# Permuted tokens, densely written block transposes, and strip tiles moved into the closing sums' buffer, in a decoder layer on one Trainium2 core

## The chip, the cores and the metric

The kernel runs on one core of one Trainium2 chip. Its time is the device time of one launch in microseconds, and a kernel's time is the median of its runs. PE is the matmul engine, DVE and ACT the vector and the scalar engine, POOL the general engine, and SP here only issues DMAs. POOL and ACT issue DMAs too. Each engine works through its own queue of instructions in the order in which they were put there.

## The reference, cut to what matters

One layer of a decoder, 256 tokens of width 2048, all in float32:

```
h  = rmsnorm(x) ; p = h @ W_in                        # 2048 -> 3 x 1024 + 512 + 512 + 64
A  = 8 heads, causal dilated windows (128,1), (512,4), (2048,16), partial rotary, merged by softmax denominators
B  = 8 heads, latent attention with rotary part, causal
x  = x + rmsnorm(concat(A, B) @ W_out)
u  = square(relu(rmsnorm(x) @ W_up))                  # 2048 -> 8192
x  = x + rmsnorm(u @ W_down)                          # 8192 -> 2048
```

The gains of the norms are left out above. Positions enter through the rotary parts and the causal masks alone; everything else treats each token by itself.

## The kernel before, in words

**Matmuls.** The tokens form two blocks of 128 (`b` = 0, 1), one token per partition. Each float32 operand of a matmul is split into a high part (`hi`, an ACT copy that rounds, L310; for W_up with the gain, L314) and a low part (`lo`, the rest, on DVE, L311 and L315), and PE adds three products of 128x128 by 128x512 for each block of a product (L300). Weight tiles of 128x1024 arrive as `raw` by DMAs that SP issues (L194), and are split on ACT and DVE before PE uses them. Some pairs of row tiles go through a scheme of seven products instead of eight: POOL loads both tiles as one transfer of 1 MB (L378, into `ab`, `ab2`, later `ab_down`, `u` and `c`), DVE forms the sums of weights (L365 to L370, into `st_down`, `t`, `u`), and these too are split. The products go to banks `m` (up) or `md` (down).

**Up projection.** The outer loop has eight stages `j`; each makes 1024 columns of W_up's result for both blocks, that is, the strips 2j and 2j+1 of 512 columns. At a stage's end `close` (L1095 and L1098) turns the banks `m` into four tiles of 128x512 in the buffer `c` (the closing sums, 128x2048), which are then added to the four accumulators (L1160). In the next stage `up_evac` takes each accumulator: ACT applies relu and the square into a tile `r` (L941, L942; three buffers with the tag "r"), and a DMA on ACT's queue writes `r` to memory as `rkeep`, with its pieces permuted (L944). `turn_u` reads it back as `x` (L953, also in the "r" buffers), and DVE transposes it in blocks of 32x32 (STREAM_TRANSPOSE, L962) into `uT`, the transposed strip that the down projection uses on the stationary side. For strips 4 to 13, `lo_away` puts the low part of `uT` in memory ahead of time: ACT writes a negated rounded copy `neg` (L976, again in the "r" buffers), ACT's queue sends it to `ukeep` (L978), POOL later adds `uT` to it by an accumulating DMA (L988), and the down projection loads it as `ulo` (L1018).

**Down projection.** It starts at 707.7 us with strips that are ready, while the last strips are still being evacuated. For each strip, `uhi` and `ulo` are made by ACT and DVE (`split`, L310 and L311) or, for strips 4 to 13, by ACT (L1001) and the load. The seven-products steps load their weights into `ab_down`, `u` or `c`; `c`, the former closing buffer, is used by five of these loads, the first one soon after the start. Near the end `x_back` loads the residual x (`xkeep`) into the space of four old strips (L1212, four DMAs on SP) and scales it by `pwi` (L1217).

**The order.** A Python object (`Flow`) keeps a clock that advances with each matmul put into PE's queue. Work beside the matmuls is written as chains that give the number of units (us of that clock) until they go on; when the clock reaches a chain's due time, its next instructions are appended to their engines' queues. So delays in the code, such as `D_BACK`, `D_TURN` and `D_LO`, set places in the queues, not times on the chip. Weight tiles are appended so many tiles ahead of their use (`W_AHEAD` = 6).

```
nc.vector.transpose(uT[j][:, :, b * P:(b + 1) * P].rearrange("p k (t q) -> p k q t", q=4),
                    x.rearrange("p (q k c) -> p k q c", q=4, k=4))
if j in AWAY:
    flow.start(lo_away(j), 1.0)
```

Of the kernel before, what the change touches and what calls it, by code (L numbers as in the profile page):

```python
# [53 lines left out]

def shape_constants():

    fa = (THETA ** (-np.arange(0, RA, 2, dtype=np.float64) / RA)).astype(np.float32)
    fb = (THETA ** (-np.arange(0, RB, 2, dtype=np.float64) / RB)).astype(np.float32)
    freq = np.concatenate([-fa, fa, -fb, fb, fa, fa, fb, fb])
    i = np.arange(P)[:, None] + P  # L60
    j = np.arange(2 * P)[None, :]
    dist = i - j
    count = np.zeros((P, 2 * P))
    for window, dil in CONFIGS:
        count += (dist >= 0) & (dist <= window) & (dist % dil == 0)
    bias_a = np.where(count > 0, np.log(np.maximum(count, 1)) / SCALE_A, NEG)
    bias_b = np.where(dist >= 0, 0.0, NEG)
    out = np.concatenate([np.broadcast_to(freq, (P, 192)), bias_a, bias_b], axis=1)
    return np.ascontiguousarray(out.astype(np.float32))
# [24 lines left out]

D_BACK, D_LAST, D_TURN, D_LO, D_ADD = 12.0, 6.0, 9.0, 4.0, 23.0

# [171 lines left out]
def layer(nc, tc, io):  # L268
# [570 lines left out]
    pw, pwi = [con.tile([P, NB], F32, name=n) for n in ("pw", "pwi")]  # L839
    pws = con.tile([P, 4, NB], F32, name="pws")  # L840
    xkeep = [dram.tile([P, D], F32, name=f"xkeep{b}") for b in range(NB)]

    def powers():
# [11 lines left out]
        nc.vector.tensor_single_scalar(out=pwi.bitcast(I32), in_=pw.bitcast(I32), scalar=0x7F800000, op=OP.bitwise_xor)  # L855
        nc.vector.tensor_scalar_mul(pwi, pwi, 0.5)
        for i, (v, c) in enumerate(((pwi, 1.0 / D), (pwi, EPS), (pw, EPS))):
            nc.vector.scalar_tensor_tensor(out=pws[:, i, :], in0=v, scalar=c, in1=v, op0=OP.mult, op1=OP.mult)
# [78 lines left out]
    def up_evac(j, b, acc, order):  # L937
# [7 lines left out]
                            in_=r.rearrange("m (a c) -> m a c", a=4))  # L945
        flow.start(turn_u(j, b, keep), D_BACK + D_LAST * (b and j % 2))

    turned = set()

    def turn_u(j, b, keep):  # L950

        x = late["up"].tile([P, 512], F32, tag="r", bufs=3, name=f"x{j}_{b}")
        nc.scalar.dma_start(out=x, in_=keep)  # L953
        yield D_TURN
        if j not in uT:
            if j in (0, 1, 10, 11, 12, 13):
                t2 = late["u01" if j < 2 else "ab2" if j < 12 else "ab"][:, j % 2 * CW:(j % 2 + 1) * CW]
            else:
                tag = {"tag": "T", "bufs": 2} if j > 13 else {"tag": f"uT{j}", "bufs": 1}
                t2 = late["up"].tile([P, CW], F32, name=f"uT{j}", **tag)  # L960
            uT[j] = t2.rearrange("p (k s) -> p k s", k=4)
        nc.vector.transpose(uT[j][:, :, b * P:(b + 1) * P].rearrange("p k (t q) -> p k q t", q=4),  # L962
                            x.rearrange("p (q k c) -> p k q c", q=4, k=4))
        if b:
            turned.add(j)
            if j in AWAY:
                flow.start(lo_away(j), 1.0)

# [238 lines left out]
    def x_back():  # L1207

        for b in range(NB):
            for i in range(2):  # L1210
                x = uT[6 + 2 * b + i].rearrange("p k s -> p (k s)")
                nc.sync.dma_start(out=x, in_=xkeep[b][:, i * CW:(i + 1) * CW])  # L1212
        yield 20.0
        for b in range(NB):
            for i in range(2):
                x = uT[6 + 2 * b + i].rearrange("p k s -> p (k s)")
                nc.vector.tensor_scalar_mul(x, x, pwi[:, b:b + 1])  # L1217
                yield 1.5
# [117 lines left out]
def arrays_of(inputs):  # L1336

    a = {n: np.ascontiguousarray(inputs[n][0]) for n in ("x", "w_in", "w_uq", "w_ukv", "w_out", "w_up", "w_down")}
    a["xt"] = np.ascontiguousarray(np.concatenate([a["x"], inputs["norm_attn_pre"]]).T)
    a["pos"] = np.ascontiguousarray(inputs["positions"].reshape(NB, P).T)  # L1340
    a["gains"] = np.ascontiguousarray(np.concatenate(
# [3 lines left out]
    for n in ("norm_attn_post", "norm_mlp_post"):  # L1345
        a[n] = np.ascontiguousarray(inputs[n])
    a["consts"] = shape_constants()
    return a
# [20 lines left out]
```

## Time and profile before

| | us |
|---|---|
| runs | 1061.3, 1063.65, 1061.65 (median 1061.65) |
| profiled execution, its own time | 1060.02 |
| its span, first to last instruction | 1058.2 |
| busy: PE, DVE, ACT, POOL | 1030.5, 842.7, 638.7, 74.8 |
| mean granted clock of PE | 0.991 |

In rows of the profile, "out<-in" names what an instruction writes and reads, followed by its size; a bracket at a row's end gives the idle time of that engine just before it and what ended it. A row of a window's table gives the window, its length, and for PE, PEld (weight loads of PE), DVE, ACT and POOL the busy time with the count of instructions, then the granted clock, the share of busy DMA engines and GB/s. A row of waits gives engine and instruction, what it waited for, the total, how many times, and the longest. A row of a tile gives a form with its count, the least, median and largest duration in ns, and the first and last start. In a chain, start, length and what it was.

### The profile page before, as it was taken

What the parts mean: (1) busy time and instruction counts of PE and PEld (TensorE: products, weight loads), DVE (VectorE), ACT (ScalarE), POOL (GpSimd) and SP (SyncE); (2) the same over time, 40 slices, a digit from 0 to 9 for tenths busy, and PEclk for the clock granted to TensorE, in tenths of its full rate; (3) what the DMA queues carried; (4) which work ended last, traced back from release to release, by engine and by line L of the source; (5) the groups of instructions that cost most, each with busy time, mean ns of one, the idle gap of its engine ahead of it and who ended that gap; (6) DMA issues with size and microseconds to landing.
All of it is one profiled execution on the core that took longest, in us unless ns stands there. A gap on an engine that the chain in (4) does not pass through costs nothing.

```text
span 1058.2 us, 13302 instructions
## 1 busy us (share of the span) xinstructions
PE 1030.5 (97%) x4715; PEld 853.2 (81%) x4715; DVE 842.7 (80%) x1125; ACT 638.7 (60%) x862; POOL 74.8 (7%) x114
## 2 busy tenths in 40 slices
PE   9999999999999999999999999896999999999996
PEld 6888899888888788888887768685888888888885
DVE  6676546577556679999989889894999999989795
ACT  6675446565454567676575676665576665767561
POOL 0000000000000000000010100010210100121100
PEclk9999999999999999999999999998999999999998
DMA  8975547454356298777898988779979868889962
GB/s 303 363 232 151 147 122 229 149 170 156 123 197 221 92 366 264 233 258 231 271 275 270 307 236 270 208 266 328 310 268 379 299 216 302 284 312 328 365 235 80
DMA packets 108099, 259.74 MB, mean 245 GB/s; under 512 B 8704, under 2 KB 29696, under 8 KB 107648
## 3 DMA queue, kind: packets, MB, share of 16 engines
q1 hardware_dynamic: 64144, 169.90, 47.7%
q0 software_dynamic: 19072, 66.59, 19.6%
q10 hardware_dynamic: 24816, 22.40, 6.5%
q8 instruction: 37, 0.61, 0.2%
q14 instruction: 30, 0.25, 0.1%
HBM read 227.92 MB, written 30.93 MB: 245 GB/s over the span
## 4 chain that ended last, share of the span: by engine, by line
PE 78%; DVE 8%; DMA 5%; ACT 4%; issue 3%; ACTq 0%; SPq 0%; POOL 0%; DVEq 0%; POOLq 0%
PE y L300 22%; PE acc_u L300 14%; PE acc_o L300 8%; PE md L300 6%; PE acc_v L300 4%; PE acc_qk L300 4%; PE m L300 3%; PE acc_ckv L300 2%; DMA rkeep<-r 2%; DVE lo L315 2%; PE acc_ukv L300 2%; PE acc_q L300 2%; PE acc_cq L300 2%; PE acc_k L300 2%; DVE lo L311 2%
## 5 line engine op out<-in xcount | busy, mean ns | idle before, releaser
L311 DVE TENSOR_TENSOR lo<-raw,hi 128x1024 fp32r<-128x1024 f32 (+3 forms) x205 | 231.3, 1148 | 95.1 <-ACT hi L310 94.4
L310 ACT ACTIVATE hi<-raw 128x1024 fp32r<-128x1024 f32 (+3 forms) x205 | 201.0, 995 | 66.4 <-DMA raw<-in_w_in 17.1
L300 PE MATMUL acc_u<-lo,hT_hi 128*128 128x512 f32 x386 | 152.1, 394 | 6.9 <-DVE lo L315 6.9
L300 PE MATMUL acc_u<-hi,hT_hi 128*128 128x512 f32 x386 | 153.0, 396 | 2.1 <-DVE c L1098 1.4
L300 PE MATMUL acc_u<-hi,hT_lo 128*128 128x512 f32 x386 | 151.5, 392 | 0.4 <-DVE hT_lo L311 0.4
L300 PE MATMUL y<-hi,uhi 128*128 128x512 f32 x352 | 137.8, 392 | 7.8 <-ACT uhi L310 7.8
L300 PE MATMUL y<-hi,ulo 128*128 128x512 f32 x352 | 137.7, 391 | 0.2 <-DVE ulo L311 0.2
L300 PE MATMUL y<-lo,uhi 128*128 128x512 f32 x352 | 137.7, 391 | 0.0
L315 DVE SCALAR_TENSOR_TENSOR lo<-raw,gcol,hi 128x1024 fp32r<-128x1024 f32 x86 | 106.4, 1267 | 16.6 <-ACT hi L314 16.6
L314 ACT ACTIVATE hi<-raw,gcol 128x1024 fp32r<-128x1024 f32 x86 | 96.2, 1145 | 31.4 <-DMA raw<-in_w_up 14.1
L300 PEld LDWEIGHTS acc_u<-lo,hT_hi 128*128 128x128 f32 x386 | 73.3, 190 | 23.2 <-DVE lo L315 8.3
L300 PEld LDWEIGHTS acc_u<-hi,hT_hi 128*128 128x128 f32 x386 | 73.1, 189 | 20.0 <-DVE c L1098 3.6
L300 PEld LDWEIGHTS acc_u<-hi,hT_lo 128*128 128x128 f32 x386 | 73.3, 190 | 16.3 <-DVE hT_lo L311 0.9
L300 PEld LDWEIGHTS y<-hi,uhi 128*128 128x128 f32 x352 | 66.5, 189 | 22.0 <-ACT uhi L310 8.2
L300 PEld LDWEIGHTS y<-hi,ulo 128*128 128x128 f32 x352 | 66.5, 189 | 14.8 <-DVE ulo L311 0.9
L300 PEld LDWEIGHTS y<-lo,uhi 128*128 128x128 f32 x352 | 66.5, 189 | 13.8 <-DVE lo L311 0.2
L311 DVE TENSOR_TENSOR lo<-st_down,hi 128x1024 fp32r<-128x1024 f32 x48 | 57.5, 1219 | 0.6 <-ACT hi L310 0.6
L310 ACT ACTIVATE hi<-st_down 128x1024 fp32r<-128x1024 f32 x48 | 49.6, 1050 | 5.3 <-DVE st_down L370 3.9
L300 PE MATMUL md<-hi,s 128*128 128x512 f32 x144 | 52.1, 389 | 0.0
L300 PE MATMUL acc_o<-hi,mixT_hi 128*128 128x512 f32 x128 | 51.8, 405 | 0.0
L300 PE MATMUL acc_o<-hi,mixT_lo 128*128 128x512 f32 x128 | 50.2, 392 | 0.0
L300 PE MATMUL acc_o<-lo,mixT_hi 128*128 128x512 f32 x128 | 50.0, 390 | 0.0
(331 smaller groups left out, 2037.4 us busy)
## 6 DMA issues: line engine op xcount, KB each, us to landing
raw<-in_w_up SPq DMA_DIRECT2D x86, 512.0 KB, 5.1
raw<-in_w_down SPq DMA_DIRECT2D x80, 512.0 KB, 6.7
raw<-in_w_in SPq DMA_DIRECT2D x55, 512.0 KB, 5.1
ab<-in_w_up POOLq DMA_DIRECT2D x17, 1024.0 KB, 6.5
raw<-in_w_out SPq DMA_DIRECT2D x32, 512.0 KB, 4.4
ab_down<-in_w_down POOLq DMA_DIRECT2D x13, 1024.0 KB, 8.5
ulo<-ukeep POOLq DMA_DIRECT2D x25, 512.0 KB, 6.9
rkeep<-r ACTq DMA_DIRECT2D x32, 256.0 KB, 3.5
```

The lines of the kernel that those rows point to most:

```text
L300: nc.tensor.matmul(out, a, b, start=start, stop=stop)
L310: nc.scalar.activation(hi, src, AF.Copy)
L311: nc.vector.tensor_tensor(out=lo, in0=src, in1=hi.bitcast(F32), op=OP.subtract)
L314: nc.scalar.activation(hi, src, AF.Copy, scale=g)
L315: nc.vector.scalar_tensor_tensor(out=lo, in0=src, scalar=g, in1=hi.bitcast(F32), op0=OP.mult, op1=OP.subtract)
```

## The change

It has four parts.

- *Token order.* The host permutes the tokens within each block of 128: position 4t + q holds token 32q + t. The rows of x, its transpose, the positions and both masks follow. The block transposes then write, for each of four pieces of a strip, 128 elements side by side (`(q t)`), where they wrote with a step of four elements (`(t q)`). The rows of `uT` that the down projection uses are in natural order, and so is the output.
- *The residual's way back.* x in memory is in the permuted order and the output isn't, so `x_back` loads it in 16 pieces of 32 rows in place of four loads of 128 rows, with 2.0 units between groups of four. The factor `pwi` is written to memory by POOL (`pwk`) and read back in order as `pwn` by four small DMAs on SP.
- *The strips' tiles.* The tile that is read back (`x`) is no longer one of the three "r" buffers, but a quarter of `c`: strips 2j and 2j+1 of block `b` take the quarters 2b and 2b + 1.
- *Delays.* `D_BACK` 12 to 8 and without the 6 more that one tile of a stage had, `D_TURN` 9 to 8, the start of `lo_away` 1 to 9 (`D_NEG`), `D_LO` 4 to 2, `D_ADD` 23 to 25.

```diff
--- before.py
+++ after.py
@@ -52,7 +52,7 @@
 C3 = float(np.float32(2 * np.pi - C1 - C2))
 
 
-def shape_constants():
+def shape_constants(order):
 
     fa = (THETA ** (-np.arange(0, RA, 2, dtype=np.float64) / RA)).astype(np.float32)
     fb = (THETA ** (-np.arange(0, RB, 2, dtype=np.float64) / RB)).astype(np.float32)
@@ -65,6 +65,7 @@
         count += (dist >= 0) & (dist <= window) & (dist % dil == 0)
     bias_a = np.where(count > 0, np.log(np.maximum(count, 1)) / SCALE_A, NEG)
     bias_b = np.where(dist >= 0, 0.0, NEG)
+    bias_a, bias_b = [m[order[:P]][:, order] for m in (bias_a, bias_b)]
     out = np.concatenate([np.broadcast_to(freq, (P, 192)), bias_a, bias_b], axis=1)
     return np.ascontiguousarray(out.astype(np.float32))
 
@@ -92,7 +93,7 @@
 
 UP_STEP = 2.4
 
-D_BACK, D_LAST, D_TURN, D_LO, D_ADD = 12.0, 6.0, 9.0, 4.0, 23.0
+D_BACK, D_TURN, D_NEG, D_LO, D_ADD = 8.0, 8.0, 9.0, 2.0, 25.0
 
 
 SUMS_AHEAD = 2
@@ -838,6 +839,7 @@
 
     pw, pwi = [con.tile([P, NB], F32, name=n) for n in ("pw", "pwi")]
     pws = con.tile([P, 4, NB], F32, name="pws")
+    pwk, pwn = dram.tile([P, NB], F32, name="pwk"), con.tile([P, NB], F32, name="pwn")
     xkeep = [dram.tile([P, D], F32, name=f"xkeep{b}") for b in range(NB)]
 
     def powers():
@@ -854,6 +856,7 @@
         nc.vector.tensor_single_scalar(out=pw.bitcast(I32), in_=r.bitcast(I32), scalar=0x7F800000, op=OP.bitwise_and)
         nc.vector.tensor_single_scalar(out=pwi.bitcast(I32), in_=pw.bitcast(I32), scalar=0x7F800000, op=OP.bitwise_xor)
         nc.vector.tensor_scalar_mul(pwi, pwi, 0.5)
+        nc.gpsimd.dma_start(out=pwk, in_=pwi)
         for i, (v, c) in enumerate(((pwi, 1.0 / D), (pwi, EPS), (pw, EPS))):
             nc.vector.scalar_tensor_tensor(out=pws[:, i, :], in0=v, scalar=c, in1=v, op0=OP.mult, op1=OP.mult)
         for b in range(NB):
@@ -943,13 +946,13 @@
         keep = dram.tile([P, 512], F32, name=f"rkeep{j}_{b}")
         nc.scalar.dma_start(out=keep.rearrange("(a t) (q c) -> (t q) a c", a=4, q=4),
                             in_=r.rearrange("m (a c) -> m a c", a=4))
-        flow.start(turn_u(j, b, keep), D_BACK + D_LAST * (b and j % 2))
+        flow.start(turn_u(j, b, keep), D_BACK)
 
     turned = set()
 
     def turn_u(j, b, keep):
 
-        x = late["up"].tile([P, 512], F32, tag="r", bufs=3, name=f"x{j}_{b}")
+        x = closing()[2 * b + j % 2]
         nc.scalar.dma_start(out=x, in_=keep)
         yield D_TURN
         if j not in uT:
@@ -959,12 +962,12 @@
                 tag = {"tag": "T", "bufs": 2} if j > 13 else {"tag": f"uT{j}", "bufs": 1}
                 t2 = late["up"].tile([P, CW], F32, name=f"uT{j}", **tag)
             uT[j] = t2.rearrange("p (k s) -> p k s", k=4)
-        nc.vector.transpose(uT[j][:, :, b * P:(b + 1) * P].rearrange("p k (t q) -> p k q t", q=4),
+        nc.vector.transpose(uT[j][:, :, b * P:(b + 1) * P].rearrange("p k (q t) -> p k q t", q=4),
                             x.rearrange("p (q k c) -> p k q c", q=4, k=4))
         if b:
             turned.add(j)
             if j in AWAY:
-                flow.start(lo_away(j), 1.0)
+                flow.start(lo_away(j), D_NEG)
 
     def lo_away(g):
 
@@ -1206,15 +1209,22 @@
 
     def x_back():
 
+        def in_order(rows):
+            return rows.rearrange("(t q) d -> q t d", q=4)
+
+        for q in range(4):
+            nc.sync.dma_start(out=pwn[32 * q:32 * q + 32], in_=in_order(pwk)[q])
         for b in range(NB):
             for i in range(2):
                 x = uT[6 + 2 * b + i].rearrange("p k s -> p (k s)")
-                nc.sync.dma_start(out=x, in_=xkeep[b][:, i * CW:(i + 1) * CW])
+                for q in range(4):
+                    nc.sync.dma_start(out=x[32 * q:32 * q + 32], in_=in_order(xkeep[b])[q, :, i * CW:(i + 1) * CW])
+                yield 2.0
         yield 20.0
         for b in range(NB):
             for i in range(2):
                 x = uT[6 + 2 * b + i].rearrange("p k s -> p (k s)")
-                nc.vector.tensor_scalar_mul(x, x, pwi[:, b:b + 1])
+                nc.vector.tensor_scalar_mul(x, x, pwn[:, b:b + 1])
                 yield 1.5
 
     def load_gain(n, out):
@@ -1336,15 +1346,17 @@
 def arrays_of(inputs):
 
     a = {n: np.ascontiguousarray(inputs[n][0]) for n in ("x", "w_in", "w_uq", "w_ukv", "w_out", "w_up", "w_down")}
+    order = np.concatenate([b * P + 32 * (np.arange(P) % 4) + np.arange(P) // 4 for b in range(NB)])
+    a["x"] = np.ascontiguousarray(a["x"][order])
     a["xt"] = np.ascontiguousarray(np.concatenate([a["x"], inputs["norm_attn_pre"]]).T)
-    a["pos"] = np.ascontiguousarray(inputs["positions"].reshape(NB, P).T)
+    a["pos"] = np.ascontiguousarray(inputs["positions"].reshape(S)[order].reshape(NB, P).T)
     a["gains"] = np.ascontiguousarray(np.concatenate(
         [inputs[n].reshape(-1, P) for n in ("q_latent_norm", "kv_latent_norm", "norm_mlp_pre")]).T)
     a["w_down"] = np.ascontiguousarray(
         a["w_down"].reshape(FF // 512, 4, 4, 32, D).transpose(0, 2, 1, 3, 4).reshape(FF, D))
     for n in ("norm_attn_post", "norm_mlp_post"):
         a[n] = np.ascontiguousarray(inputs[n])
-    a["consts"] = shape_constants()
+    a["consts"] = shape_constants(order)
     return a
 
 
```

The order of PE's instructions is the same in both kernels. Three places of the other queues:

ACT in the sixth stage, where strips 8 and 9 are read back (`x8`, `x9`, and in the change `c`) and the first negated copy of strip 8 is made. L314, L310 and L953, L976, L978 of before are L315, L311 and L956, L979, L981 of the change. Before:

```order
L310 ACTIVATE hi244_5377<-t5_2_5317 128x1024
L314 ACTIVATE hi245_5392<-raw245_5390,gcol_69 128x1024
L314 ACTIVATE hi246_5404<-raw246_5402,gcol_69 128x1024
L953 DMA x9_1_5412<-rkeep9_1_5236 128x512
L976 ACTIVATE neg8_0_5425<-uT8_5372 128x512
L314 ACTIVATE hi247_5432<-raw247_5430,gcol_69 128x1024
L978 DMA ukeep8_5424<-neg8_0_5425 128x512
L314 ACTIVATE hi248_5445<-raw248_5443,gcol_69 128x1024
L314 ACTIVATE hi249_5457<-raw249_5455,gcol_69 128x1024
```

and in the change:

```order
L956 DMA c_3507<-rkeep9_1_5223 128x512
L311 ACTIVATE hi241_5329<-ab_3505 128x512
L311 ACTIVATE hi242_5347<-ab_3505 128x1024
L311 ACTIVATE hi243_5354<-u5_2_5304 128x1024
L311 ACTIVATE hi244_5365<-t5_2_5303 128x1024
L315 ACTIVATE hi245_5377<-raw245_5375,gcol_69 128x1024
L315 ACTIVATE hi246_5391<-raw246_5389,gcol_69 128x1024
L315 ACTIVATE hi247_5414<-raw247_5412,gcol_69 128x1024
L315 ACTIVATE hi248_5427<-raw248_5425,gcol_69 128x1024
L979 ACTIVATE neg8_0_5438<-uT8_5324 128x512
L315 ACTIVATE hi249_5442<-raw249_5440,gcol_69 128x1024
L981 DMA ukeep8_5437<-neg8_0_5438 128x512
```

The last read-back is now ahead of four `hi` of `ab`, `u` and `t`, and the negated copy has moved back by two weight tiles, from directly behind the read-back to nine rows behind it.

DVE about 40 us into the down projection, where strips 14 and 15 are transposed and the first sums over `c` are formed. Before (L962 is the transpose, L365 to L370 the sums, L1032 to L1034 sums for strip 5):

```order
L962 STREAM_TRANSPOSE uT14_6528<-x14_1_6490 128x4x4x32
L311 TENSOR_TENSOR s0_9_6564<-st_down_6292,s0_9_6564 128x512
L311 TENSOR_TENSOR lo308_6568<-st_down_6292,hi308_6567 128x1024
L365 TENSOR_TENSOR st_down_6292<-c_3504 128x1024
L369 TENSOR_TENSOR st_down_6292<-st_down_6292,c_3504 128x512
L370 TENSOR_TENSOR st_down_6292<-st_down_6292,c_3504 128x512
L311 TENSOR_TENSOR lo309_6590<-raw309_6587,hi309_6589 128x1024
L311 TENSOR_TENSOR lo310_6614<-raw310_6611,hi310_6613 128x1024
L311 TENSOR_TENSOR lo311_6634<-c_3504,hi311_6633 128x512
L962 STREAM_TRANSPOSE uT15_6539<-x15_1_6558 128x4x4x32
L311 TENSOR_TENSOR lo312_6643<-c_3504,hi312_6642 128x1024
```

and in the change (L965 the transpose, L366 to L371 the sums):

```order
L965 STREAM_TRANSPOSE uT14_6465<-c_3507 128x4x128
L1035 TENSOR_TENSOR st_down_6269<-uT4_4580 128x256
L1036 TENSOR_TENSOR st_down_6269<-st_down_6269,uT4_4580 128x128
L1037 TENSOR_TENSOR st_down_6269<-uT4_4580,st_down_6269 128x128
L312 TENSOR_TENSOR lo307_6520<-st_down_6269,hi307_6519 128x1024
L965 STREAM_TRANSPOSE uT15_6481<-c_3507 128x4x128
L312 TENSOR_TENSOR s0_9_6536<-st_down_6269,s0_9_6536 128x512
L312 TENSOR_TENSOR lo308_6540<-st_down_6269,hi308_6539 128x1024
L366 TENSOR_TENSOR st_down_6269<-c_3507 128x1024
L370 TENSOR_TENSOR st_down_6269<-st_down_6269,c_3507 128x512
L371 TENSOR_TENSOR st_down_6269<-st_down_6269,c_3507 128x512
```

The last transpose of strip 15, which stood six rows behind the first sum over `c`, now stands three rows ahead of it, and it reads from `c`, as the three others do. So POOL's load into `c`, which stands at the same place in POOL's queue relative to the `ab_down` loads, has these transposes ahead of it.

SP near the end, where x is brought back, before:

```order
L194 DMA raw442_8618<-in_w_down 128x1024
L1212 DMA uT6_4994<-xkeep0_2445 128x1024
L1212 DMA uT7_5010<-xkeep0_2445 128x1024
L1212 DMA uT8_5372<-xkeep1_2446 128x1024
L1212 DMA uT9_5388<-xkeep1_2446 128x1024
L194 DMA raw447_8683<-in_w_down 128x1024
L194 DMA raw448_8705<-in_w_down 128x1024
L194 DMA raw453_8766<-in_w_down 128x1024
```

and in the change:

```order
L195 DMA raw442_8589<-in_w_down 128x1024
L1216 DMA pwn_2446<-pwk_2445 32x2 x4
L1221 DMA uT6_4950<-xkeep0_2447 32x1024 x4
L1221 DMA uT7_4965<-xkeep0_2447 32x1024 x4
L1221 DMA uT8_5324<-xkeep1_2448 32x1024 x4
L195 DMA raw447_8666<-in_w_down 128x1024
L1221 DMA uT9_5339<-xkeep1_2448 32x1024 x4
L195 DMA raw448_8692<-in_w_down 128x1024
L195 DMA raw453_8753<-in_w_down 128x1024
```

Each "x4" row is four DMAs; twenty DMAs stand where four stood, and one weight tile (`raw447`) has moved ahead of the last group.

## The prediction, made before the changed kernel had run

> **What bounds the kernel now.** I read the page's busy times first, then the same length of span in two places, then what PE waited for.
>
> ```profile
> PE 1030.5 (97%) x4715; PEld 853.2 (81%) x4715; DVE 842.7 (80%) x1125; ACT 638.7 (60%) x862; POOL 74.8 (7%) x114
> 540.00:760.00 220.00, 202.71 (x855) 162.81 (x855) 187.99 (x206) 136.76 (x163) 21.41 (x26) 0.97 0.88 274
> 800.00:1020.00 220.00, 220.00 (x972) 182.09 (x971) 203.50 (x230) 145.33 (x165) 28.72 (x48) 1.00 0.86 310
> PE y L300 <- ACT uhi L310: 7.8, 1, 7.8
> PE acc_u L300 <- DVE lo L315: 6.9, 4, 3.5
> PE acc_u L300 <- DVE c L1098: 1.4, 4, 0.4
> ```
>
> PE's matmuls fill 97% of the span, and the order of PE's instructions does not change, so only time in which PE fails to start a matmul can be won. The two windows are both 220 us long. In 800 to 1020 PE starts 972 matmuls without a gap, one every 220/972 = 0.226 us. In 540 to 760 (the second half of the up projection and the first of the down projection) it starts 855, so 117 × 0.226 = 26.5 us are missing. That is the ground on which the change acts. The waits of PE name three releasers: one wait of 7.8 at the start of the down projection, and in the up stages the weights' low parts (`lo`, 6.9) and the closing sums (`c`, 1.4).
>
> The wait of 7.8, matmul by matmul:
>
> ```profile
> 729.19 0.39 PE L300 MATMUL y<-hi,ulo 128*128 128x512 f32 x1
> 737.35 0.79 PE L300 MATMUL y<-hi,uhi 128*128 128x512 f32 x1 [7.78 <-ACT uhi L310]
> 741.10 0.63 PE L300 MATMUL y<-lo,uhi 128*128 128x512 f32 x1
> 741.84 0.40 PE L300 MATMUL y<-hi,uhi 128*128 128x512 f32 x1
> ```
>
> The matmul at 741.84 is the tenth after the one at 729.19 and was due at 729.19 + 10 × 0.227 = 731.46: the place costs 10.4 us, of which 8.2 is the gap and 2.2 the matmuls after it, which take 0.63 instead of 0.39 until 741.84. That tail I add to each long stall below. Of the 26.5 this leaves 16.1 for the up stages.
>
> ACT runs its queue in order, and at this place it stood behind a transfer:
>
> ```profile
> 715.54 15.10 DMA rkeep<-r
> 730.72 0.69 ACT L941 ACTIVATE r<-acc_u,rstd_pre 128x512 f32<-128x512 f32 x1 [7.50 <-DMA rkeep<-r]
> 736.26 1.04 ACT L310 ACTIVATE uhi<-uT 128x1024 fp32r<-128x1024 f32 x1
> ```
>
> The last strip's `r` needs one of three buffers, whose write to memory took 15.1 us; `uhi` of strip 2, which PE needs, is queued behind it. Now a stage of the up projection, with ACT's waits in it:
>
> ```profile
> 577.00:622.00 45.00, 42.84 (x187) 34.31 (x186) 40.74 (x45) 28.48 (x35) 7.26 (x9) 1.00 0.94 289
> ACT neg L976 <- DVE uT L962: 9.1, 2, 6.2
> ACT hi L314 <- DMA rkeep<-r: 2.5, 1, 2.5
> ACT r L941 <- DMA ukeep<-neg: 2.0, 2, 1.7
> 607.49 0.63 ACT L976 ACTIVATE neg<-uT 128x512 fp32r<-128x512 f32 x1 [6.16 <-DVE uT L962]
> 618.98 0.63 ACT L310 ACTIVATE hi<-ab 128x512 fp32r<-128x512 f32 x1 [0.46 <-ACT neg L976]
> ```
>
> A stage is 183 matmuls, 183 × 0.227 = 41.5 us; this one lasted 45.0. DVE works 40.7 of it. ACT works 28.5, but is held for 9.1 + 2.5 + 2.0 = 13.6, and its eight DMA issues cost about 0.45 each (the last row stands behind one, idle 0.46), 3.6 together: 45.7, the length of the stage. So I take ACT's queue, not its work, as what stretches these stages: the negated copies (`neg`) stand in it before their transposes are done, the weights' `hi` wait behind them, DVE's `lo` waits for `hi`, and PE for `lo`.
>
> **The change part by part.** *Dense transposes.* The token order makes DVE write 128 elements in a row where it wrote single elements 16 bytes apart.
>
> ```profile
> L962 DVE STREAM_TRANSPOSE uT<-x x20: 1046/1078/1134, 469.1 to 760.4; 128x512 f32<-128x512 f32 x20
> L660 DVE COPY qkT_a<-qkT_a x8: 680/691/692, 74.8 to 175.4; 128x512 f32<-128x512 f32 x8
> L1217 DVE TENSOR_SCALAR uT<-uT,pwi x4: 750/751/753, 1016.7 to 1022.7; 128x1024 f32<-128x1024 f32 x4
> ```
>
> A dense transpose of this size does not occur before. Its bounds are 1.08 (nothing won) and 0.38, half of the 751 ns for twice the elements in one pass; nearest is a copy of the same 128x512 in 0.69, which I take. A stage has four: 4 × 0.39 = 1.6 us less on DVE, 40.7 → 39.1, against PE's 41.5. It reads the same strided input either way.
> The Trainium skill says ("SBUF — State Buffer", section on the DMA port swizzle) that accesses which leave a 16-byte line pay a penalty; the old pattern leaves it at each element, which agrees in direction with 1.08 against 0.69, and gives no price of its own.
>
> *Negated copies 8 units later, strips' tiles out of the three `r` buffers.* The copies now stand behind their transposes in ACT's queue, which removes the 9.1, and without the strips' tiles three buffers serve eight allocations a stage instead of twelve. What remains for ACT: 28.5 + 3.6 + about 4 (2.5 + 2.0 less a little) = 36, below PE's 41.5 by 5. But the last transpose of a stage has to be done before the closing sums, whose buffer it reads, and was behind them until now; a late tile stops DVE. How late:
>
> ```profile
> DMA to landing us min/median/max: 2.7/5.0/11.0
> DMA to landing us min/median/max: 2.3/4.1/15.1
> ```
>
> These are the loads of the strips' tiles and the transfers on the tile `rkeep` (both directions), issue to landing. The tiles are now asked for 4 to 10 units earlier, so a write of 10 holds the load's issue for some 2 us, and a load of 11 exceeds the 8 units given by 3. I put 3.1 us for all the remaining stages together: **13.0 of the 16.1 come back** (bounds: 0 and 16.1).
>
> *The down projection's start.* By the rows, without the 7.50 `uhi` ends at 736.26 + 1.04 − 7.50 = 729.80, against 729.42 when PE needs it: 0.4 us late, plus some for two tile loads now issued ahead of it, which wait for their writes. I take 1.5 lost, so **8.9 of 10.4 come back**. The wait is still there in the program (the fourth `r` needs the first one's buffer); what makes it short is that the burst on POOL around the write thins out:
>
> ```profile
> 708.12 0.73 POOL L378 DMA_DIRECT2D ab_down<-in_w_down  x1 [37.22 <-PE acc_u L300]
> 708.85 2.67 POOL L988 DMA_DIRECT2D ukeep<-ab  x3
> 715.18 0.73 POOL L378 DMA_DIRECT2D c<-in_w_down  x1 [3.67 <-ACT r L941]
> ```
>
> The load of 1 MB into `c` at 715.18 must now wait, and one of the accumulating writes goes elsewhere. If the write takes 15.1 all the same, nothing comes back: bounds 0 and 10.4.
>
> *The new wait.* That load of `c` has to wait, since strips 14 and 15 lie in `c` until their transposes are done. The rows:
>
> ```profile
> 734.84 0.42 ACTq L944 DMA_DIRECT2D rkeep<-r  x1
> 752.09 1.12 DVE L962 STREAM_TRANSPOSE uT<-x 128x512 f32<-128x512 f32 x1
> 754.89 1.23 DVE L365 TENSOR_TENSOR st_down<-c 128x1024 f32<-128x1024 f32 x1
> 757.49 2.35 DVE L311 TENSOR_TENSOR lo<-raw,hi 128x1024 fp32r<-128x1024 f32 x2
> 761.09 5.44 PE y L300 x24
> DMA to landing us min/median/max: 9.1/10.6/17.2
> ```
>
> In time without the stall of 10.4, the last transpose, now in the place of the row at 752.09, ends at 752.09 − 10.4 + 0.7 = 742.4. POOL issues the load then, and the last row (the loads of `c`) gives 10.6: it lands at 753.0. The sums over `c` stand next in DVE's queue, 757.49 − 754.89 = 2.6, until 755.6; behind them is the `lo` of an ordinary weight tile, about 1.2, until 756.8. The 24 matmuls which use it are due at 761.09 − 10.4 = 750.7. So PE stalls 6.1 (4.6 with a landing of 9.1) and pays the 2.2 of the slow restart: **8.3 new**. With 17.2 it is 14.9. `ulo` of strip 4, an accumulating write and the next `ab_down` are queued behind this load on POOL; their uses follow closely, and I add **1.0** for them.
>
> *The way back of x.* Four loads of 512 KB become 16 of 128 KB and four tiny ones on SP, the multiply takes `pwn`.
>
> ```profile
> 973.46 1.81 SPq L1212 DMA_DIRECT2D uT<-xkeep  x4
> uT<-xkeep SPq DMA_DIRECT2D x4, 512.0 KB, 8.7
> 993.84 1.23 DVE L365 TENSOR_TENSOR st_down<-ab_down 128x1024 f32<-128x1024 f32 x1 [6.10 <-DMA ab_down<-in_w_down]
> 996.43 2.35 DVE L311 TENSOR_TENSOR lo<-raw,hi 128x1024 fp32r<-128x1024 f32 x2
> 997.73 5.47 PE y L300 x24
> ```
>
> Twenty issues at the 0.45 of these four (1.81/4) are 9 us on SP instead of 1.8; weight loads behind them move by some 7. SP runs well ahead of PE's use here, so I set 0. The edge is `ab_down`: DVE waits 6.10 for it, and the `lo` behind its sums ends about 0.1 before PE needs it at 997.73 (996.43 + 1.2). Whatever delays that load further is paid in full; bounds 0 and 8.7, a second such load's time.
>
> *Nothing:* tokens, positions and masks are permuted on the host; the copy of `pwi` to memory is one tiny DMA on POOL, hundreds of us ahead of its use.
>
> **The sum**, against the profiled execution's own 1060.02: −13.0 − 8.9 + 8.3 + 1.0 = −12.6 → 1047.4. The runs' median lies 1.6 above that execution: **1049**.
>
> **The rivals.** *A: the new wait is hidden.* If the tiles arrive early enough, or DVE reaches the transposes sooner than in the old order, `c` lands before its sums are due. For it: strips 14 and 15 have nothing between write and load but DMA. Against: 10.6 for the load alone, with PE's due time only 8.3 after the transpose. Without the 8.3 and the 1.0: 1060.02 − 21.9 + 1.6 = 1040.
>
> *B: the stages stretch for another reason.* If `hi` and `lo` are late because all evacuation work falls together at a stage's end, moving `neg` gains little, and only DVE's 1.6 in each of the four late stages returns, 6.4 instead of 13.0: 1049 + 6.6 = 1056. For it: DVE is at 40.7 of 41.5 already. Against: early stages had the same evacuations and no loss.
>
> ```profile
> 410.00:451.00 41.00, 41.00 (x183) 33.95 (x182) 40.25 (x44) 25.66 (x29) 2.15 (x3) 1.00 0.75 248
> ```
>
> *C: the pieces on 32 partitions.* Each of the 16 pieces reaches a quarter of the partitions; if they move slower than one whole load, they crowd `ab_down`. For it: the margin of 0.1. Against: the same bytes, spread over a longer time. If `ab_down` lands later by the 7.2 us (9 − 1.8) that the issues stretch, they fall on PE: 1056.
> The Trainium skill ("SBUF — State Buffer", "Can I just issue two DMAs to hit both halves?") says a transfer picks its ports by its own span of partitions; its table has 189 GB/s for 32 partitions against 328 for 128. By that ratio of 1.7 the four loads would take 0.7 × 8.7 = 6 us longer each, an estimate, and the time would be about 1055. No row of before has a load of 32 partitions.
>
> *D: slower.* The chain from the last `r` to `c` meets slow transfers throughout. Its write, 734.84 − 7.5 = 727.3, lands 15.1 later at 742.4, the tile's load 11.0 later at 753.4, the transpose ends at 754.1, `c` lands 17.2 later at 771.3, the `lo` is there at 775.1 against 750.7: a stall of 24.4 + 2.2 = 26.6, 18.3 over the forecast: 1067. It decides against the change once the chain is 13 us longer than I take it. For it: each of these durations has occurred, and the traffic there is heavy. Against: never three in a row.
>
> *E: no change.* The `r` write takes 15.1 again, so that nothing comes back at `uhi`, and B holds too: −6.4 + 8.3 + 1.0 = +2.9, 1064.6; but the stall at `uhi` gives `c` time and hides about 3 of the 8.3, which leaves 1062.
>
> **How the numbers follow.** Forecast 0.47 (1045 to 1053), A 0.15, B 0.14, C 0.10, D 0.09, E 0.05. A difference of less than 0.2%, 2 us, cannot be told here. Faster: 0.47 + 0.15 + 0.14 + 0.10 = 0.86; same 0.05; slower 0.09. The range holds A's inner half, B and C: 1038 to 1060.
>
> **What would show it.** In the changed profile: transposes of 0.69; no wait of ACT's `neg` for transposes; a stage of 41.5 to 42.5 us in 577 to 667; PE's wait for `uhi` under 2; a POOL wait of the first `c` load for the last transpose, and DVE idle 5 to 9 us before `st_down<-c`, with PE stalled behind it some 43 us after the down projection starts (750.7 − 707.7). I am wrong in the up stages if ACT is not held and PE still waits for `lo`; wrong in the down start if `c` lands before DVE asks for it; wrong on x if DVE's 6.10 for `ab_down` grows.

## The result, and the profile after

| | us |
|---|---|
| changed kernel, median of 20 runs | 1063.54 (1062.46 to 1068.73) |
| kernel before, median of 20 runs | 1061.55 (1060.31 to 1063.65) |
| ratio | 1.0024, 95% interval 1.0015 to 1.0033 |
| profiled execution of the changed kernel: own time, span | 1065.99, 1064.2 |

The change makes the kernel slower by a quarter of a per cent; 1049 was forecast, with 1038 to 1060 as the range. The profiled execution is one of the slower ones, 2.4 over the median, and it is the one taken apart here: its span is 6.0 longer than that of before.

PE's part of the page, the two windows of the prediction, and PE's waits, of the changed kernel:

```profile
PE 1038.5 (98%) x4715; PEld 855.0 (80%) x4715; DVE 833.6 (78%) x1125; ACT 639.2 (60%) x862; POOL 74.4 (7%) x115
540.00:760.00 220.00, 208.51 (x888) 169.06 (x886) 179.00 (x202) 136.06 (x163) 24.37 (x30) 0.98 0.87 274
800.00:1020.00 220.00, 218.84 (x963) 180.33 (x962) 200.03 (x227) 140.72 (x160) 28.69 (x48) 1.00 0.87 308
PE y L301 <- DVE lo L312: 6.5, 2, 5.3
PE acc_u L301 <- DVE lo L316: 6.3, 3, 3.4
PE y L301 <- ACT uhi L311: 1.9, 1, 1.9
```

In 540 to 760 PE now starts 888 matmuls instead of 855: 33 × 0.2267 = 7.5 us are won there. The wait for `uhi` is 1.9 instead of 7.8, and a wait of 5.3 for `lo` at a place that had none is the new one behind `c`. So the span should have become shorter. But PE is busy for 8.0 us more with the same 4715 matmuls, and in 800 to 1020, where it lost nothing before, it starts 963 instead of 972. About six of these nine are one stall, at 1012, behind the way back of x; the others, with PE busy throughout, are not.

Where it is busy longer, a window early in the program shows, more than 250 us ahead of the first instruction that the change adds or moves in a queue (the write of `pwk`, at 325.7). Of the kernel before and of the changed kernel, 20 to 60 us:

```profile
20.00:60.00 40.00, 40.00 (x178) 33.14 (x177) 28.58 (x40) 26.90 (x34) 0.00 (x0) 1.00 0.96 330
L300 PE MATMUL acc_v<-hi,xT_hi x64: 389/389/389, 49.7 to 144.8; 128*128 128x512 f32 x64
L300 PE MATMUL m<-hi,st x84: 388/389/393, 417.0 to 701.3; 128*128 128x512 f32 x84
```

```profile
20.00:60.00 40.00, 40.00 (x174) 32.11 (x173) 28.67 (x39) 27.49 (x35) 0.00 (x0) 1.00 0.96 337
L301 PE MATMUL acc_v<-hi,xT_hi x64: 393/395/397, 50.7 to 147.8; 128*128 128x512 f32 x64
L301 PE MATMUL m<-hi,st x84: 393/396/397, 422.5 to 703.5; 128*128 128x512 f32 x84
L301 PE MATMUL acc_u<-hi,hT_hi x386: 387/389/628, 359.7 to 709.1; 128*128 128x512 f32 x193
```

PE is full in both and the granted clock is 1.00 in both, yet 40 us hold 174 matmuls instead of 178. The groups of matmuls tell which (least, median, largest duration in ns): those whose stationary tile is xT or the sums `st` take 395 and 396, the one with hT takes 389, as the groups did before. By the starts of consecutive matmuls the slow ones follow each other at 0.2333 us, the others at 0.2267.

From the starts of all 4715 matmuls I split the time that PE loses: a distance above 0.26 us counts as a stall, one of 0.229 to 0.26 as pace, both less 0.2267. The stalls before the up projection are 9 to 11 in every kernel and left out. A row's pace depends by about half a us on where these limits are put, the differences between rows hardly do. "Up" is the up projection, "uhi" the start of the down projection, "c" the place behind the first load into `c`, "rest" what comes later. The experiments' rows, which follow below, stand in the same table (median of all runs; the other columns from one profiled execution):

| kernel | median | span | up | uhi | c | rest | pace |
|---|---|---|---|---|---|---|---|
| before | 1061.5 | 1058.2 | 15.7 | 10.4 | 0.0 | 0.0 | 1.7 |
| changed | 1063.54 | 1064.2 | 10.9 | 4.6 | 7.3 | 1.4 | 9.8 |
| e1: changed, no tile moved | 1057.62 | 1053.8 | 6.2 | 6.2 | 8.4 | 0.8 | 1.8 |
| e2: before, left side moved by 32 bytes | 1068.51 | 1066.9 | 15.9 | 10.2 | 0.0 | 0.0 | 9.9 |
| e3: before, moved by 64 bytes | 1064.12 | 1060.5 | 14.8 | 10.5 | 0.0 | 0.0 | 5.3 |
| e5: e1, last transposes earlier | 1052.38 | 1048.6 | 6.6 | 4.8 | 1.3 | 2.9 | 1.6 |
| e6: e1 without tiles in `c` and delays | 1055.49 | 1054.3 | 10.4 | 10.3 | 0.0 | 1.0 | 1.7 |
| e7: before with tiles in `c` and delays | 1064.43 | 1062.7 | 13.9 | 5.6 | 9.7 | 0.0 | 1.8 |
| e8: e5, POOL's writes later | 1046.38 | 1045.9 | 2.6 | 6.8 | 0.8 | 3.4 | 1.5 |
| e9: e5, copies 5 units after | 1050.33 | 1046.9 | 4.8 | 5.4 | 1.3 | 3.4 | 1.7 |
| e10: e8, last writes later | 1045.32 | 1043.6 | 1.3 | 6.4 | 0.2 | 3.5 | 1.6 |
| e11: e10 and e9, pieces spread | 1044.74 | 1045.0 | 0.0 | 5.2 | 0.0 | 7.3 | 1.7 |
| e12: e8, x in whole loads | 1045.34 (one run) | 1043.5 | 0.4 | 6.2 | 0.8 | 2.5 | 1.4 |
| e13: before, POOL's writes later | 1060.52 | 1059.2 | 16.1 | 10.5 | 0.0 | 0.0 | 1.8 |

For the changed kernel against before: −4.8 − 5.8 + 7.3 + 1.4 + 8.1 = +6.2, the span's difference of 6.0 within 0.2. Without the 8.1 of pace the change would have been a gain.

The lines that answer to the prediction's steps, of the changed kernel: the transposes, ACT's waits in 460 to 710, a piece of the chain of waits, and DVE and PE behind the load into `c`:

```profile
L965 DVE STREAM_TRANSPOSE uT<-c x20: 697/704/711, 470.8 to 748.1; 128x512 f32<-128x512 f32 x20
ACT hi L315 <- DMA raw<-in_w_up: 14.6, 6, 4.7
ACT r L944 <- DMA ukeep<-neg: 14.6, 4, 4.6
ACT hi L311 <- DMA rkeep<-r: 14.1, 4, 5.7
585.09 13.99 DMA rkeep<-r
599.47 1.06 ACT L311 ACTIVATE hi<-t 128x1024 fp32r<-128x1024 f32 x1 [5.74 <-DMA rkeep<-r]
748.10 0.70 DVE L965 STREAM_TRANSPOSE uT<-c 128x512 f32<-128x512 f32 x1
749.10 0.73 POOL L379 DMA_DIRECT2D c<-in_w_down  x1 [36.30 <-DMA ukeep<-ulo]
759.11 1.23 DVE L366 TENSOR_TENSOR st_down<-c 128x1024 f32<-128x1024 f32 x1 [8.60 <-DMA c<-in_w_down]
762.98 0.80 PE L301 MATMUL y<-lo,uhi 128*128 128x512 f32 x1 [5.35 <-DVE lo L312]
```

A transpose takes 0.70 (0.69 was taken). ACT's waits of `neg` for transposes, 40.2 in these 250 us before, are gone, but three others have grown to 14 or 15: for weights that have not landed (6.7 before), for the copies' own writes (3.5), and for the writes of `r` that the read-backs in ACT's queue wait for (5.3). In all, ACT is idle there for 84.6 us instead of 88.4. The last transpose ends at 748.8 and the load into `c` goes out at 749.1 (the profile names a landing at 749.08 as its releaser, which ended 0.3 later than the transpose; e5 below tells the two apart).

### The profile page after: what moved, and what is told of

Its sections match the earlier page's. It is cut to its first block, busy times and chain, and to the rows that moved or that the text cites. A ratio compares the mean times of both kernels' runs of the same rounds, so it can differ in the third digit from the quotient of the medians.

```text
span 1064.2 us, 13304 instructions
## 1 busy us (share of the span) xinstructions
PE 1038.5 (98%) x4715; PEld 855.0 (80%) x4715; DVE 833.6 (78%) x1125; ACT 639.2 (60%) x862; POOL 74.4 (7%) x115
## 4 chain that ended last, share of the span: by engine, by line
PE 71%; DMA 12%; DVE 7%; ACT 4%; issue 3%; ACTq 1%; POOL 0%; SPq 0%; DVEq 0%; POOLq 0%
PE y L301 19%; PE acc_u L301 12%; PE acc_o L301 8%; PE md L301 5%; PE acc_v L301 4%; PE acc_qk L301 4%; DMA ukeep<-neg 3%; DMA rkeep<-r 3%; DVE lo L312 2%; PE acc_ckv L301 2%; PE acc_q L301 2%; PE acc_k L301 2%; PE acc_cq L301 2%; PE acc_ukv L301 2%; PE m L301 2%
## 5 line engine op out<-in xcount | busy, mean ns | idle before, releaser
L311 ACT ACTIVATE hi<-raw 128x1024 fp32r<-128x1024 f32 (+3 forms) x205 | 201.2, 995 | 71.9 <-DMA raw<-in_w_in 16.7
L315 ACT ACTIVATE hi<-raw,gcol 128x1024 fp32r<-128x1024 f32 x86 | 97.2, 1148 | 39.3 <-DMA raw<-in_w_up 20.0
L311 ACT ACTIVATE hi<-st_down 128x1024 fp32r<-128x1024 f32 x48 | 49.9, 1052 | 4.9 <-DVE st_down L371 3.9
```

Source lines behind the costliest of these rows:

```text
L311: nc.scalar.activation(hi, src, AF.Copy)
L315: nc.scalar.activation(hi, src, AF.Copy, scale=g)
```

## The experiments

The kernel before was run again beside each group of experiments; its medians there are 1061.4 to 1061.5, and the ratios below are to these.

**The pace: is it the place of the tiles?** In the built programs every tile on the left side of SBUF (the weights' `hi` and `lo`, hT, `uhi`, `ulo`) lies 32 bytes higher in the changed kernel: the new small tile `pwn` stands below them. Those on the right (xT, mixT, `st`, some of the second pass's `ulo`) have not moved. The slow matmuls are those with the moving tile on the left and the stationary one on the right. e1 takes the shift away:

```diff
-    pw, pwi = [con.tile([P, NB], F32, name=n) for n in ("pw", "pwi")]
+    pw, pwin = con.tile([P, NB], F32, name="pw"), con.tile([P, 2, NB], F32, name="pwin")
+    pwi, pwn = pwin[:, 0, :], pwin[:, 1, :]
-    pwk, pwn = dram.tile([P, NB], F32, name="pwk"), con.tile([P, NB], F32, name="pwn")
+    pwk = dram.tile([P, NB], F32, name="pwk")
```

> The changed kernel with pwi and pwn packed into one small tile, so that every tile lies at the address it has in the kernel before; nothing else is changed. In the changed kernel's profile the matmuls up to 360 us start every 0.2333 us instead of 0.2267, as do those with the sums st and half of the second pass's low parts; the new tile pwn had moved all tiles on the left side of SBUF (weights, hT, uhi, ulo) by 32 bytes against those on the right (xT, mixT, st). Theory 1, the shift does this: all matmuls are back at 0.2267, the time falls by 7.7 us, from 1063.5 to about 1056. Theory 2, the permuted tokens or the execution do it: the matmuls up to 360 us stay at 0.2333 and the time at 1063.5.

e2 gives the kernel before the shift alone (`con.tile([P, 8], F32, name="shift")` behind `pws`), e3 twice as much (`[P, 16]`):

> The kernel before with an unused tile of 32 bytes behind pws, which moves the left side by 32 bytes and changes nothing else. Theory 1 (shift): matmuls up to 360 us at 0.2333, slower by about 7.7 us: 1069. Theory 2 (tokens or execution): 1061.6.

> The kernel before with an unused tile of 64 bytes at the same place. If what counts is whether the moving and the stationary tile lie alike within 64 bytes: 0.2267 and 1061.6, as before. If any shift of the left against the right side costs: 0.2333 and about 1069.

Measured: e1 1057.62 (ratio to before 0.9957, 0.9942 to 0.9972), e2 1068.51 (1.0063, 1.0049 to 1.0077), e3 1064.12 (1.0023, 1.0013 to 1.0033). The same window and the same two groups, of e1, then e2, then e3:

```profile
20.00:60.00 40.00, 40.00 (x178) 33.10 (x178) 27.82 (x40) 26.59 (x34) 0.00 (x0) 1.00 0.96 331
L301 PE MATMUL acc_v<-hi,xT_hi x64: 389/389/389, 49.8 to 144.9; 128*128 128x512 f32 x64
L301 PE MATMUL m<-hi,st x84: 389/389/389, 417.1 to 691.8; 128*128 128x512 f32 x84
```

```profile
20.00:60.00 40.00, 40.00 (x173) 32.15 (x172) 29.33 (x40) 28.06 (x37) 0.00 (x0) 1.00 0.96 342
L300 PE MATMUL acc_v<-hi,xT_hi x64: 393/395/397, 51.2 to 148.4; 128*128 128x512 f32 x64
L300 PE MATMUL m<-hi,st x84: 389/396/397, 423.0 to 709.3; 128*128 128x512 f32 x84
```

```profile
20.00:60.00 40.00, 40.00 (x177) 32.82 (x176) 29.57 (x41) 27.78 (x36) 0.00 (x0) 1.00 0.97 339
L300 PE MATMUL acc_v<-hi,xT_hi x64: 388/390/392, 50.3 to 145.9; 128*128 128x512 f32 x64
L300 PE MATMUL m<-hi,st x84: 389/392/397, 418.4 to 702.2; 128*128 128x512 f32 x84
```

e1 has the permuted tokens and the old pace, e2 the old tokens and the slow pace: the shift does it, not the data and not the execution. It costs 7.0 us in the kernel before (e2) and 5.9 in the changed one. e3 lies between: neither of its expectations held. The matmuls take 390 and 392 in the median, their starts lie from 0.226 to 0.232 apart, and the time is 2.6 over before.

**The load into `c`.** e5 is e1 with `yield 3.0 if j > 13 else D_TURN` in place of `yield D_TURN` in `turn_u`.

> e1 with the transposes of strips 14 and 15 due 3 units after their read-back instead of 8, so that POOL's first load into c, which waits for them, can start earlier. In the changed kernel the last tile has landed at 737.1 but is transposed at 748.1, the load goes out at 749.1, lands at 759.0, and PE stalls 5.3 (7.3 with the slow restart). Theory, the place of the transposes in DVE's queue holds the load: PE's wait there falls below 1.5 us and the time by 5 to 7 us against e1, to about 1050. Rival, the load is slow whenever it goes out, since it meets the accumulating writes: a gain of 0 to 2, about 1055.

Measured 1052.38 (0.9913, 0.9895 to 0.9932), 5.2 under e1. POOL's and DVE's rows of e5:

```profile
735.21 0.73 POOL L379 DMA_DIRECT2D c<-in_w_down  x1 [32.87 <-DVE uT L966]
743.67 1.22 DVE L366 TENSOR_TENSOR st_down<-c 128x1024 f32<-128x1024 f32 x1 [2.65 <-DMA c<-in_w_down]
```

Here the load's releaser is the transpose, and DVE waits 2.65 instead of 8.60 behind it; PE's loss at this place falls from 8.4 to 1.3. The theory holds: the place of the transposes in DVE's queue held the load. Another 2 us appear a little later (in "rest"), where PE now waits for the next low part and the next `ulo`.

**What shortens the up stages?** e6 and e7 each have half of the change. e6: token order, dense transposes, pieces of x, with `pwn` packed as in e1; tiles and delays as before. e7, from the kernel before:

```diff
-D_BACK, D_LAST, D_TURN, D_LO, D_ADD = 12.0, 6.0, 9.0, 4.0, 23.0
+D_BACK, D_TURN, D_NEG, D_LO, D_ADD = 8.0, 8.0, 9.0, 2.0, 25.0
-        flow.start(turn_u(j, b, keep), D_BACK + D_LAST * (b and j % 2))
+        flow.start(turn_u(j, b, keep), D_BACK)
-        x = late["up"].tile([P, 512], F32, tag="r", bufs=3, name=f"x{j}_{b}")
+        x = closing()[2 * b + j % 2]
-                flow.start(lo_away(j), 1.0)
+                flow.start(lo_away(j), D_NEG)
```

> Token order, dense transposes, the residual's way back in pieces, and all tiles at their old addresses; the strips' tiles are again in the three r buffers and all delays are those of before. Theory of the prediction (the queue of ACT, in which the negated copies stand ahead of their transposes, stretches the up stages): a transpose takes 0.70 instead of 1.08, but ACT's wait for it stays, so of PE's 15.7 us of stalls in the up stages at most 3 go, the 10.4 at uhi stay, the pieces cost 1: about 1060. Rival (DVE's load stretches the stages): 1.5 us in each of the four late stages, 1056.

> The kernel before with the strips' tiles in c and the new delays alone; tokens, transposes and the residual's way back as before, no tile moved. Theory of the prediction: the gain in the up stages comes from here; PE's stalls there fall from 15.7 to 6 to 8 (6.2 in e1), at uhi from 10.4 to 5 to 6, and the load into c costs 8 to 9: about 1058. Rival (dense transposes make the gain): the up stages keep 12 or more, and with the 8 for c it is slower than before, 1063 or more.

Measured: e6 1055.49 (0.9948, 0.9931 to 0.9964), e7 1064.43 (1.0025, 1.0014 to 1.0035). ACT's largest waits in 460 to 710, of e6 and then of e7:

```profile
ACT neg L980 <- DVE uT L966: 21.1, 6, 5.2
ACT neg L980 <- DVE ab L966: 14.7, 4, 5.2
```

```profile
ACT hi L314 <- DMA raw<-in_w_up: 20.9, 11, 4.5
ACT hi L310 <- PE acc_u L300: 12.7, 11, 2.1
ACT r L941 <- DMA ukeep<-neg: 11.6, 3, 4.0
```

This goes against the prediction's theory in both. In e7 ACT's waits for transposes are down from 40.2 to 1.1, and PE's stalls in the up stages fall only from 15.7 to 13.9: ACT waits for the next thing that is late, and is idle for 86.7 us in 460 to 710 where it was idle for 88.4. In e6 36 us of waits for transposes remain, and the stalls fall to 10.4, by 1.3 in the mean of four stages, close to the 1.5 that DVE saves. Both together (e1) give 6.2, which is 2.4 more than the two gains added. For the total the rivals had the better numbers, 1056 and 1063 or more.

So the shorter transposes alone give about half of the gain, and moving the copies behind their transposes gives little by itself. That DVE's work is what stretches the stages is not shown by this. The shorter transposes also end sooner, and ACT's waits for them fall by 4.4 in e6, about as much as PE's stalls; and e7's delays bring new waits for transfers into ACT's queue (11.6 for the copies' writes, 3.5 before), which may hide what the move is worth. e7 with those writes out of the way was not run. Why DVE should set the pace at 40.7 of 45 us is argued only: PE wants each `lo` at its place, and raw buffers come free behind DVE's `lo`.

**The writes of `r`.** e8 is e5 with `D_ADD` 40 instead of 25, e13 the kernel before with 40 instead of 23:

> e5 with D_ADD 40 in place of 25: the four accumulating writes of a stage move behind POOL's next load of 1 MB, off the time in which ACT writes r to memory. Theory: rkeep is slow (12 to 16 us for the third and fourth tile of a stage) because these four writes and the load are issued just ahead of it; now it takes 8 at most, ACT's wait for it (5.5 in the sixth stage) goes, PE's stalls in the up stages fall from 6.6 to 4 or less, and the runs scatter less than e5's 1049 to 1056: about 1050. Rival: the load alone is enough to slow rkeep, or the read-back now meets the writes: no gain, 1052 or more.

> The kernel before with D_ADD 40 in place of 23 and nothing else. Theory: the slow writes of r behind POOL's accumulating writes also cost the kernel before; PE's stalls in the up stages fall from 15.7 to about 11 to 13, the 10.4 at uhi stay: 1058 to 1060. Rival: there the copies and transposes set the stages anyway: 1061.5.

Measured: e8 1046.38 (0.9859, 0.9844 to 0.9874), 6.0 under e5 (2.7 between the profiled executions); e13 1060.52 (0.9991, 0.9982 to 1.0000), with 16.1 in the up stages. The writes do get faster in both: the third and fourth of the sixth stage take 5.9 and 3.6 us in e8 (8.7 and 12.5 in e5), and 5.2 and 3.2 in e13 (10.8 and 9.6 before). The theory holds for the changed kernel and falls for the one before. There the read-back comes 12 to 18 units after the write, and a write of 10 us does not matter much; with 8 units the read-back stands in ACT's queue and holds it, by 14.1 in all in the changed kernel. In e8 ACT waits for such a write once in 460 to 710, for 0.5, and PE's stalls in the up stages are down to 2.6. e8's four runs lie closer together (1045.4 to 1047.7) than e5's six (1049.4 to 1056.1), but e10's five, with the same `D_ADD`, go from 1043.6 to 1048.8; that the slow writes made the scatter is not shown.

**The copies.** e9 is e5 with `D_NEG` 5 and `D_ADD` 29.

> e5 with the negated copies 5 instead of 9 units after the transpose and D_ADD 29, so that POOL's writes keep their place. Theory: with 9 the copies' own writes come so late that the next stage's r, which needs their buffers, waits for them (15.5 us of ACT's waits in the changed kernel, 5.4 in before); with 5 that wait falls below 6 and PE's stalls in the up stages from 6.6 to 5 or less: 1050 to 1051. Rival: the stalls at the stages' ends come from the weights' raw loads and the evacuation itself: 1052 as e5.

Measured 1050.33 (0.9897, 0.9882 to 0.9912), 2.1 under e5, with 4.8 instead of 6.6 in the up stages: the theory's size and direction, though the intervals of e5 and e9 overlap.

**The start of the down projection, and the pieces of x.** e10 is e8 with `yield 24.0 + ...` in place of `4.0 + ...` for the writes of strips 10 to 13. e11 adds e9's copies (`D_NEG` 5, `D_ADD` 44) and 6.0 units instead of 2.0 between the groups of pieces, 12.0 instead of 20.0 behind them. e12 is e8 with four whole loads of x; it adds the residual to other tokens' rows and serves for its trace alone.

> e8 with the accumulating writes of strips 10 to 13 20 units later. Theory: PE's stall at uhi (6.8 us in e8, 4.6 to 6.2 in the other variants) is what is left of the slow writes of the last r tiles, which these writes slow from POOL; with them later, the writes take 8 at most, the stall falls below 3, the time by 3 to 5 us: 1042. Rival: POOL's load of 1 MB into ab_down at that place is enough to slow them: 1046 as e8.

> e10 with the negated copies 5 units after the transpose (D_ADD 44 keeps POOL's writes in place) and with the 16 pieces of x spread further, 6.0 instead of 2.0 units between groups of four. Theory: up stages as in e9, 1 to 2 us less than e10; at the end the 1.7 us that PE loses behind ab_down go, since the pieces no longer crowd that load: together 2 to 3 us under e10, about 1040. Rival: both gains overlap with what e8 and e10 gave: as e10.

> e8 with the residual brought back in four loads of 128 rows as before; its rows are then in permuted order, so that part of the result is left out (the residual is added to other tokens' rows). Theory: the 1.7 us that PE loses near 994 in e8 come from the pieces; PE's wait there is below 0.3 and ab_down lands as early as in before relative to its issue (15 us). Rival: they come from the shifted phase of the whole, and stay.

Measured: e10 1045.32 (0.9850, 0.9834 to 0.9867), e11 1044.74 (0.9842, 0.9828 to 0.9855), e12 1045.34 in its one execution. POOL's rows and a piece of the chain of waits of e10 at the start of the down projection:

```profile
693.44 0.74 POOL L379 DMA_DIRECT2D ab_down<-in_w_down  x1 [62.48 <-PE acc_u L301]
694.17 1.79 POOL L992 DMA_DIRECT2D ukeep<-ab  x2
704.28 12.92 DMA rkeep<-r
```

e10 missed: the loss at `uhi` stays at 6.4. Two accumulating writes still went out behind `ab_down` there, so it doesn't tell whether these or the load of 1 MB keep the writes of `r` at 13 us; that stays open. In e11 the up stages lose nothing any more, but the end loses more. DVE's waits in 960 to 1003, of e8 and of e12, and PE's waits of e11:

```profile
DVE st_down L366 <- DMA u<-in_w_down: 5.5, 1, 5.5
DVE st_down L366 <- DMA ab_down<-in_w_down: 3.9, 1, 3.9
```

```profile
DVE st_down L366 <- DMA ab_down<-in_w_down: 6.0, 1, 6.0
DVE st_down L366 <- DMA u<-in_w_down: 0.9, 1, 0.9
```

```profile
PE y L301 <- DVE lo L312: 3.8, 2, 3.3
PE y L301 <- ACT uhi L311: 3.0, 1, 3.0
```

With whole loads the 1.7 us that e8 loses near 994 are gone, so they come from the pieces; the kernel before, e7 and e13, which have whole loads too, lose nothing there either. The load that is late is not `ab_down` but the next one, into `u`: issued while pieces are still in flight, it lands 16.8 us later in e8 and 10.5 in e12, and DVE's wait for it is 5.5 against 0 (e12's 0.9 belongs to an earlier load), while `ab_down` lands sooner in e8 (12.6) than in e12 (14.9). Spread further (e11), the pieces are in flight until 992.8, the load into `u` takes 18.6, and the place costs 5.2 instead of 1.7: e11's second expectation was wrong. e11 and e10 are equal within their intervals. Either is 1.5% faster than the kernel before; up stages as in e11 with pieces as in e10 were not run.

## Why the prediction was wrong

**The first step that failed** is the one that costs the rest at nothing. `pwn` was counted as four tiny DMAs; as a tile of 8 bytes a partition it moved the whole left side of SBUF by 32 bytes against the right, and every matmul that reads one operand from each side lost 6.6 ns: 8.1 us in the profiled execution, 5.9 in the medians. None of the rivals had it, and no row of the profile of before could have shown it; only the places of the tiles in the two programs do. The code has unused tiles named `con_pad`, `mix_pad` and `pa_pad`, which I read past.

**The second step that failed** is the term of the up stages, and in the profiled execution it weighs as much: −13.0 was forecast, −4.8 came, 8.2 short against the 8.1 of the pace. Without the shift (e1) the median is 1057.62: inside the range, but 8.6 over the forecast and near rival B's 1056, so the shift alone does not explain the miss.

**The terms**, with e1, where the shift is gone (spans: 1053.8 − 1058.2 = −4.4):

| term | forecast | e1 | changed |
|---|---|---|---|
| up stages | −13.0 | −9.5 | −4.8 |
| `uhi` | −8.9 | −4.2 | −5.8 |
| load into `c` | +8.3 | +8.4 | +7.3 |
| its followers | +1.0 | 0 | 0 |
| way back of x | 0 | +0.8 | +1.4 |
| pace | none | +0.1 | +8.1 |

- *Up stages.* The size was off by 3.5 in e1, and the cause is not borne out: "I take ACT's queue, not its work, as what stretches these stages" would have ACT's waits for transposes cost most of the 16.1, and with nearly all of them gone e7 won 1.8. A queue that waits as long as its stage lasts is what slack looks like too. Rival B's shorter transposes made about half of the gain (e6); by which path stays open. In the changed kernel 4.7 less came back than in e1. That is nearly all one stall, at 603, where the writes of `r` took 14.0 and 15.8 us against 11.7 and 13.0 in e1. "A write of 10 holds the load's issue for some 2 us" named this mechanism and sized it too small. Half of that stall is the slow restart, which the prediction added to each long stall as 2.2; in the runs it came after some gaps and not after others, and not simply the longer ones: starts 2.5 apart at 603 had it, 3.6 apart at 671 in e1 and 2.7 apart at 669 in e8 had not.
- *`uhi`.* Mis-sized: 0.4 + something, taken as 1.5, was 4.6 to 6.2. "What makes it short is that the burst on POOL around the write thins out" failed: the write still took 13.1 us in the changed kernel (15.1 before). The gain comes with the tiles in `c` and the delays: 5.6 are lost in e7, which has only these, and 10.3 in e6, which has the rest.
- *Load into `c`.* Right in place, cause and size (e5). Rival A did not happen: DVE reached the transposes late, not early.
- *Way back of x.* Within its bounds. Rival C's mechanism is real (e12), at 0.8 to 1.7 us instead of 7.2, but at another load: the sign to watch, DVE's 6.10 for `ab_down`, shrank to 4.2 in the changed kernel, and a wait of 5.1 for the next load, into `u`, came instead. What the Trainium skill ("SBUF — State Buffer", "Can I just issue two DMAs to hit both halves?") says of how a transfer gets its ports agrees in direction: a piece of 128 KB on 32 partitions takes 8.5 us in the median, about as long as 512 KB in one load did before (8.7). In both, several were in flight at once, so no run here has the time of a piece by itself.
- *Transposes.* 0.69 taken, 0.70 measured. The 0.69 was that of a copy, so that it fits is in part luck.

## What to carry to other kernels

When a change allocates a tile, however small, compare the addresses of all the others before pricing anything else: here 8 bytes a partition cost more than the change's own gain, and packing them into an existing slot gave it back. An engine that is held just as long as its stage lasts may be waiting because the stage is long; before taking its queue for the cause, ask what it would wait for next if that wait were gone. And a buffer that gets a second tenant brings its loads a new wait: the release has to move up in the queue together with it, as e5 did for 5 us.

## What the runs showed of the hardware that I had not expected

The pace of a 128x512 float32r matmul depends on how its moving and its stationary tile lie to each other in SBUF. In the kernel before, both lie alike within 128 bytes (`hi` of one weight tile at 67552, xT at 116704, both 96 over a multiple of 128): 0.2267 us. 32 bytes apart (e2, changed): 0.2333 for nearly all, 3% more, at a granted clock of 1.00 and without an idle row in the profile. 64 bytes apart (e3): between the two, 0.226 to 0.232. Larger or other offsets were not tried, nor was it seen which of PE's two reads yields. The Trainium skill ("SBUF — State Buffer", "Who interferes with whom") gives PE two independent read ports, one for the moving operand and one for the weight load, and says that PE never waits on anyone; the measurement differs, if only PE's own two reads are in play, and it decides.

A write of 256 KB that takes 2.3 us at best took 9 to 16 us when a load of 1 MB and two to four accumulating writes of 256 KB had gone out from POOL just ahead of it (before, changed, e5). With the load alone ahead of it, the third and fourth write of the fifth and sixth stage took 2.7 to 5.9 (e8, e13).
